# Two pools of landing buffers for weight blocks, used as one rotation in the feed-forward blocks

## The chip, the core and the metric

The kernel runs on one core of one Trainium2 chip. The metric is the device time of one execution in microseconds (us); lower is better. A time is given as the median of several runs. The profile is of one further execution, with times from the start of its first instruction.

## What is computed

The reference is a network of two layers on a sequence of 256 tokens of width 1024, in float32. Each layer is a feed-forward block, a mixer, and a second feed-forward block, each with a norm in front, a norm behind, and a residual sum:

```python
for l in range(DEPTH):                 # DEPTH = 2
    g = norm_g[l]
    h = swiglu(rms_norm(x, g[0, 0]), ffn_w_gate[l, 0], ffn_w_up[l, 0], ffn_w_down[l, 0])
    x = x + 0.5 * rms_norm(h, g[0, 1])
    h = rms_norm(x, g[1, 0])
    ...                                # m = even_mixer(h, ...) for l = 0, odd_mixer(h, ...) for l = 1
    x = x + rms_norm(m, g[1, 1])
    h = swiglu(rms_norm(x, g[2, 0]), ffn_w_gate[l, 1], ffn_w_up[l, 1], ffn_w_down[l, 1])
    x = x + 0.5 * rms_norm(h, g[2, 1])
```

with `swiglu(x, w_gate, w_up, w_down) = (silu(x @ w_gate) * (x @ w_up)) @ w_down` and an inner width of 2816. The even mixer is an attention with compressed keys and a gated recurrence, the odd one a differential attention. The kernel's six stages, in order, are block 0 (feed-forward), block 1 (even mixer), blocks 2 and 3 (feed-forward), block 4 (odd mixer) and block 5 (feed-forward).

## The kernel before

**The tokens and the products.** The 256 tokens are two tiles (`t` = 0, 1) of 128. A float32 product is made of three matmuls: each operand is split into a high part that TensorE takes at full rate and a low part, and `mm3` (lines 291 to 293) adds high x high, low x high and high x low. The first group of a stage does the same in another order (`group_first`, line 339).

**A weight block's way.** The weights lie in DRAM in the order in which they are used, cut into blocks of 128 x 1024 floats (512 KB), 331 of them. `emit_load` emits for each: a DMA by SyncE into a landing buffer `raw` (line 241), a cast by ScalarE (ACT) to the high part `whi` (line 266), a subtraction by VectorE (DVE) for the low part `wlo` (line 271). A landing buffer is free again when both have read it. `whi` and `wlo` lie in a ring of nine pairs in the feed-forward blocks (five of pool `wsp`, four of the block's pool `fw`, in the order `RING`). `fill` keeps up to seven split blocks emitted ahead of the matmuls (`AHEAD_F` + 1). The `wlo` are kept in order by a written dependency.

**A feed-forward block.** The inner width is done in six chunks (`CHUNKS`) of 512, 512, 512, 256, 512 and 512 columns, numbered 0 to 5. A chunk is gate products, then `silu` on ScalarE (line 489) from the two PSUM banks of the gate, then the transposes of the previous chunk's output (line 400), then up products into banks that the `silu` has read, then the down products of the previous chunk. The working banks are four, so the up products cannot start before the `silu`. In block 0, chunk 0's outputs `h` (line 498) and a set of sums over the turned x (`row_sums`, lines 528 to 543) are VectorE's during chunk 1.

**Kept blocks.** Chunks 2 and 4 (`SEVEN`) do gate and up with seven products in place of eight of half size: for these, VectorE forms sums of weight blocks (line 213). Eight blocks of such a chunk are kept for it: B11 (two), then T1, T2 and B21 (two each). A sum overwrites one of its operands (T1 and T2 add to B11's buffers, T3 to T1's, T4 to B21's), so a B11 buffer stays in use up to T4, the sixth of the seven operands (B11, T1, T2, B21, T3, T4, B22).

**The two pools.** `wraw` is opened once and has five landing buffers. Each feed-forward block opens `fraw` with eight (`RAWS`) in `ffn_scope`. Before the change a load is put into `fraw` if its block is one of the kept ones, into `wraw` otherwise:

```python
raw = (wraw if kind is None else state["raws"]).tile([P, SPLIT], F32, name="raw", tag="raw")
moved = nc.sync.dma_start(raw[:, :w], src[:, k * nc_:k * nc_ + w])
```

**What sets the order.** Each engine runs its own instructions in order. Their order is found when the program is built: a scheduler gives an engine, at each step of its own reckoning, the ready instruction that stands first in the program, where a load is ready when its pool has a free buffer and one of the eight DMA semaphores is to be had. So a kept block's load can be issued well before loads that stand ahead of it in the program and have no free buffer. `high_priority` puts some instructions (the splits of transposed values, the norm behind a block) ahead. `late` ties the load of two gains `g` (line 375) behind the loads of blocks 20 and 22.

**When a block's loads count as its own.** `ours` is true for a load whose block is the one whose scope is open. The first four loads of the program are emitted before block 0's scope opens; at the end of a feed-forward block the first loads of the next stage are emitted before its scope opens, and these go to `wraw`. For blocks 2 and 5 the scope opens before the last two blocks of the mixer's output weights, and these count as the feed-forward block's (`MOVED`).

Of the kernel before, what the change touches and what calls it, by code (L numbers as in the profile page):

```python
# [12 lines left out]
F32 = mybir.dt.float32  # L13
# [7 lines left out]
P = 128  # L21
# [14 lines left out]
CHUNKS = [512, 512, 512, 256, 512, 512]  # L36
SEVEN = (2, 4)
RAWS = 8
RING = "wfwfwfwfw"


# [88 lines left out]
def _unit_width(u):  # L130
    return u[3] * sum(b - a for a, b in u[4])
# [51 lines left out]
def forward(ctx, tc, a):  # L183
# [4 lines left out]
    wraw = ctx.enter_context(tc.tile_pool(name="wraw", bufs=5))  # L188
# [13 lines left out]


    SPLIT = 1024
    state = {"i": 0, "off": 0, "block": -1, "pool": None, "first": None, "n": 0, "turn": 0}
    queue = []
    los = []
    late = {}
# [3 lines left out]
    def add(to, what):  # L212
        nc.vector.tensor_tensor(to, to, what, op=ALU.add)  # L213
        return to

    def emit_load():

        if state["i"] >= len(UNITS):
            return
        u = UNITS[state["i"]]
        ours = BLOCK_OF[state["i"]] == state["block"]
        state["i"] += 1
        width = _unit_width(u)
        nk = u[3]
        kind = u[5] if len(u) > 5 else None
        if u[0] is not None:  # L230
            off = state["off"]
            state["off"] += P * width
            src = a["w"][off:off + P * width].rearrange("(p n) -> p n", p=P)
        nc_ = width // nk
        per = max(1, SPLIT // nc_)
        for k in range(0, nk, per):
            n = min(per, nk - k)
            w = n * nc_
            if u[0] is not None:
                raw = (wraw if kind is None else state["raws"]).tile([P, SPLIT], F32, name="raw", tag="raw")  # L240
                moved = nc.sync.dma_start(raw[:, :w], src[:, k * nc_:k * nc_ + w])
                for key in [key for key in late if key <= state["n"]]:
                    after(late.pop(key)(), moved)
            if kind is not None:
                if kind == "T1":
                    kept["B12", k] = raw
                    raw = add(kept["B11", k], raw)
                elif kind == "T2":
                    kept["B22", k] = raw
                    raw = add(kept["B11", k], raw)  # L250
                elif kind == "T3":
                    raw = add(kept["B12", k], kept["B22", k])
                elif kind == "T4":
                    raw = add(kept["B21", k], kept["B11", k])
                elif kind == "B22":
                    raw = kept["B22", k]
                else:
                    kept[kind, k] = raw
            pool, tag = wsp, "w"
            if ours:  # L260
                if RING[state["turn"] % len(RING)] == "f":
                    pool, tag = state["pool"], "f"
                state["turn"] += 1
            hi = pool.tile([P, SPLIT], F32R, name="whi", tag=tag + "hi")
            lo = pool.tile([P, SPLIT], F32R, name="wlo", tag=tag + "lo")
            c = nc.scalar.copy(hi[:, :w], raw[:, :w])  # L266
            if state["first"] is not None:
                if 0 < state["n"] < 16:
                    after(c, state["first"])
            state["n"] += 1  # L270
            state["lo"] = nc.vector.tensor_tensor(lo[:, :w], raw[:, :w], hi[:, :w].bitcast(F32), op=ALU.subtract)  # L271
            if los:
                after(state["lo"], los[-1])
            los.append(state["lo"])
            queue.append((hi[:, :w].rearrange("p (k n) -> p k n", k=n), lo[:, :w].rearrange("p (k n) -> p k n", k=n), n, u[2] + k))
# [27 lines left out]
    def fill():  # L303
        ahead = 3 if state["pool"] is None else state["ahead"]
        while len(queue) < ahead + 1 and state["i"] < len(UNITS):
            if state["i"] in MOVED and BLOCK_OF[state["i"]] != state["block"]:
                break
            emit_load()
# [69 lines left out]
    def after(b, a_):  # L378

        tc.add_manual_dep(b.ins, a_.ins.name, mybir.DependencyInfo(mybir.DependencyClass.NoSync, mybir.DependencyReason.SCHED_ONLY), reason="order")  # L380
# [85 lines left out]
    def ffn_scope(block):  # L466

        fx = ExitStack()
        state["pool"] = fx.enter_context(tc.tile_pool(name="fw", bufs=BUFS_F))
        state["block"] = block  # L470
        state["ahead"] = AHEAD_F
        fp = fx.enter_context(tc.tile_pool(name="fp", bufs=2))
        fr = fx.enter_context(tc.tile_pool(name="fr", bufs=4))
        state["tmp"] = lambda: fp.tile([P, 512], F32, name="tmp", tag="h")
        state["raws"] = fx.enter_context(tc.tile_pool(name="fraw", bufs=RAWS))
        state["turn"] = 0
        return fx, fp, fr

    def ffn(scope, r, turn1, gpost, gnext, at=None):
# [788 lines left out]
    with tc.tile_pool(name="pre", bufs=1) as pre:  # L1268
        lb = pre.tile([P, 512], F32, name="lb")
        lbm = pre.tile([P, 512], F32, name="lbm")  # L1270
        with tc.tile_pool(name="rt", bufs=1) as rt:
            angles, tables = rope_tables(rt, tabm, tabd)
            bounds = even_prep(lb, lbm)
            side.extend([None] * 24 + [angles, None, None, tables, None, bounds])
            r, turn1 = ffn(ffn_scope(0), r, turn1, gpost, gnext, FIRST_AT)
        gpost, gnext = load_g(0, 1, 1), load_g(0, 2, 0)
        second = even(r, turn1, tabm, lb, lbm)
    scope = ffn_scope(2)
    r, turn1 = second(gpost, gnext)
    r, turn1 = ffn(scope, r, turn1, load_g(0, 2, 1), load_g(1, 0, 0))  # L1280
    r, turn1 = ffn(ffn_scope(3), r, turn1, load_g(1, 0, 1), load_g(1, 1, 0))
    gpost, gnext = load_g(1, 1, 1), load_g(1, 2, 0)
    second = odd(r, turn1, tabd)
# [31 lines left out]
```

## Time and profile before

| | us |
|---|---|
| median of 3 runs | 1024.93 |
| lowest and highest run | 1020.07, 1025.9 |
| the profiled execution | 1024.06 |
| its span, first to last instruction | 1022.3 |

The span is that of the profiled execution alone, 1.8 us less than the execution's own time. TensorE is busy for 98% of it, VectorE for 77%, ScalarE for 57%. A busy share says little here; what matters is where TensorE stands still, and what ended that wait. In the rows below the engines are PE (TensorE, matmuls), ACT (ScalarE), DVE (VectorE), POOL (GpSimd) and SP (SyncE; SPq is its queue, which issues DMAs). L266 is line 266 of the kernel. Idle time in square brackets stands before the instruction, with the last of the things it waited for.

### The profile page before, as it was taken

To read this page: it belongs to the slowest core of one execution; us is meant where nothing else is said; L and a number is where in the kernel's file an instruction comes from. 1 tells how busy PE (TensorE), PEld (TensorE's weight loads), DVE (VectorE), ACT (ScalarE), POOL (GpSimd) and SP (SyncE) were. 2 spreads that over 40 slices of the span, in tenths; PEclk is the share of its full clock that TensorE was granted. 3 is DMA by queue.
4 is the path that set the end of the run, shared out by engine and by line. 5 is a ranking of instruction groups with operands and counts; after the bars stand their busy time and mean duration, and the time that the engine had idled before them with its cause. 6 is when DMAs were issued, how large, how long until landed. Compare 5 with 4: busy or idle time off the path is not lost.

```text
span 1022.3 us, 13231 instructions
## 1 busy us (share of the span) xinstructions
PE 996.9 (98%) x4883; PEld 828.4 (81%) x4883; DVE 789.9 (77%) x1068; ACT 584.1 (57%) x846; POOL 52.1 (5%) x61
## 2 busy tenths in 40 slices
PE   7899999999999999999999999999999989999997
PEld 6778988888788788898888789888877868889886
DVE  5888997579468789888668988865776769988852
ACT  5547575468544664747447474653665657474741
POOL 1000000022101100000000000000001200000000
PEclk8999999999899999999999999999999999999999
DMA  8948317275222873925936383494734347392431
GB/s 313 307 153 296 115 66 271 86 264 186 96 83 84 295 261 115 316 84 184 330 117 234 124 289 123 134 324 146 245 109 146 118 143 259 101 308 75 141 127 41
DMA packets 51905, 184.26 MB, mean 180 GB/s; under 512 B 6136, under 2 KB 6528, under 8 KB 51840
## 3 DMA queue, kind: packets, MB, share of 16 engines
q1 hardware_dynamic: 48960, 176.05, 50.6%
q10 hardware_dynamic: 2880, 7.37, 2.0%
q8 instruction: 38, 0.62, 0.2%
q14 instruction: 27, 0.22, 0.1%
HBM read 182.35 MB, written 1.05 MB: 179 GB/s over the span
## 4 chain that ended last, share of the span: by engine, by line
PE 84%; DVE 7%; ACT 3%; issue 3%; DMA 2%; POOL 1%; SPq 0%; DVEq 0%; POOLq 0%; ACTq 0%
PE w L291 15%; PE w L293 15%; PE w L292 15%; PE y L291 9%; PE y L293 9%; PE y L292 9%; PE w L339 6%; DMA raw<-in_w_dram 2%; DVE wlo L271 2%; PE w L400 2%; ACT whi L266 1%; PE y L400 1%; POOL pm L1153 1%; DVE E L1003 0%; PE y L929 0%
## 5 line engine op out<-in xcount | busy, mean ns | idle before, releaser
L266 ACT CAST whi<-raw 128x1024 fp32r<-128x1024 f32 (+2 forms) x379 | 392.8, 1049 | 289.2 <-PE y L293 85.1
L271 DVE TENSOR_TENSOR wlo<-raw,whi 128x1024 fp32r<-128x1024 f32 (+2 forms) x379 | 456.6, 1225 | 104.3 <-ACT whi L266 99.9
L291 PE MATMUL w<-whi,xThi 128*128 128x512 f32 (+1 forms) x676 | 254.4, 376 | 5.5 <-ACT s L489 5.5
L293 PE MATMUL w<-whi,xTlo 128*128 128x512 f32 (+1 forms) x676 | 250.8, 371 | 0.0
L292 PE MATMUL w<-wlo,xThi 128*128 128x512 f32 (+1 forms) x676 | 250.7, 371 | 0.0
L291 PEld LDWEIGHTS w<-whi,xThi 128*128 128x128 f32 x676 | 128.3, 190 | 27.9 <-ACT s L489 6.0
L293 PEld LDWEIGHTS w<-whi,xTlo 128*128 128x128 f32 x676 | 128.3, 190 | 22.4 <-issue 0.3
L292 PEld LDWEIGHTS w<-wlo,xThi 128*128 128x128 f32 x676 | 128.5, 190 | 20.8
L291 PE MATMUL y<-whi,hThi 128*128 128x512 f32 x352 | 138.6, 394 | 0.0
L293 PE MATMUL y<-whi,hTlo 128*128 128x512 f32 x352 | 137.4, 390 | 0.0
L292 PE MATMUL y<-wlo,hThi 128*128 128x512 f32 x352 | 137.4, 390 | 0.0
L213 DVE TENSOR_TENSOR raw<-raw 128x1024 f32<-128x1024 f32 x64 | 77.4, 1221 | 1.0
L293 PEld LDWEIGHTS y<-whi,hTlo 128*128 128x128 f32 x352 | 66.1, 188 | 14.4
L292 PEld LDWEIGHTS y<-wlo,hThi 128*128 128x128 f32 x352 | 66.1, 188 | 13.5
L291 PEld LDWEIGHTS y<-whi,hThi 128*128 128x128 f32 x352 | 66.1, 188 | 13.5
L408 DVE TENSOR_TENSOR hTlo<-w,hThi 128x512 fp32r<-128x512 f32 (+1 forms) x48 | 29.8, 641 | 28.3 <-ACT hThi L407 27.9
L339 PE MATMUL w<-whi,xThi 128*128 128x512 f32 (+2 forms) x124 | 39.6, 397 | 5.5 <-ACT xThi L407 5.5
L435 POOL TENSOR_TENSOR sm<-sm,mhalf 128x1 f32<-128x1 f32 x12 | 6.6, 550 | 713.2 <-DVE sm L433 713.2
L407 ACT CAST hThi<-w 128x512 fp32r<-128x512 f32 (+1 forms) x48 | 25.2, 553 | 24.5 <-PE w L400 24.5
L339 PE MATMUL w<-wlo,xThi 128*128 128x512 f32 (+2 forms) x124 | 37.7, 389 | 0.8 <-DVE wlo L271 0.8
L339 PE MATMUL w<-whi,xTlo 128*128 128x512 f32 (+2 forms) x124 | 37.9, 387 | 0.0
L489 ACT ACTIVATE s<-w,sm 128x512 f32<-128x512 f32 (+1 forms) x40 | 25.5, 645 | 13.1 <-PE w L293 12.6
(276 smaller groups left out, 1161.9 us busy)
## 6 DMA issues: line engine op xcount, KB each, us to landing
raw<-in_w_dram SPq DMA_DIRECT2D x325, 512.0 KB, 5.3
g<-in_norm_g_dram ACTq DMA_DIRECT2D x9, 512.0 KB, 5.4
raw<-in_w_dram SPq DMA_DIRECT2D x4, 448.0 KB, 3.3
g<-in_norm_g_dram SPq DMA_DIRECT2D x2, 512.0 KB, 7.9
out_dram<-x SPq DMA_DIRECT2D x4, 256.0 KB, 2.1
E<-in_hw_dram ACTq DMA_DIRECT2D x1, 576.0 KB, 6.4
x<-in_x_dram SPq DMA_DIRECT2D x2, 256.0 KB, 3.2
x<-in_x_dram SPq DMA_DIRECT2D x1, 512.0 KB
```

What stands on the lines that cost most here:

```text
L213: nc.vector.tensor_tensor(to, to, what, op=ALU.add)
L266: c = nc.scalar.copy(hi[:, :w], raw[:, :w])
L271: state["lo"] = nc.vector.tensor_tensor(lo[:, :w], raw[:, :w], hi[:, :w].bitcast(F32), op=ALU.subtract)
L291: mm(ps, hi[:, j, :], rhi, start=start, stop=False, skip_group_check=again)
L292: mm(ps, hi[:, j, :], rlo, start=False, stop=False, skip_group_check=again)
L293: state["mm"] = mm(ps, lo[:, j, :], rhi, start=False, stop=stop, skip_group_check=again)
L339: state["mm"] = mm(o, lhs[:, k, :], rhs[:, i, :], start=j == 0 and k == 0, stop=j == 2 and k == KD - 1)
L400: nc.tensor.transpose(ps[:, i * P:(i + 1) * P], src[:, (b + i) * P:(b + i + 1) * P], ident)
L407: c = nc.scalar.copy(h2, ps)
L408: return c, nc.vector.tensor_tensor(lo.rearrange("p a b -> p (a b)"), ps, h2.bitcast(F32), op=ALU.subtract)
L489: nc.scalar.activation(s[:, :w], ps[:, :w], AF.Silu, scale=r[t])
L1153: nc.gpsimd.tensor_tensor(pm[:, 1, :, :], pm[:, 1, :, :], rl.unsqueeze(2).broadcast_to([P, n, nk]), op=ALU.mult)
```

## The change

In a feed-forward block the loads are counted from the opening of its scope (`rawn`). Of each thirteen, the first five go to `wraw` and the next eight to `fraw`, whether a block is kept or not. Loads that are not the block's own go to `wraw`, as before. The pools have the sizes that they had.

```diff
--- before.py
+++ after.py
@@ -36,6 +36,7 @@
 CHUNKS = [512, 512, 512, 256, 512, 512]
 SEVEN = (2, 4)
 RAWS = 8
+RAWS_W = 5
 RING = "wfwfwfwfw"
 
 
@@ -202,7 +203,7 @@
 
 
     SPLIT = 1024
-    state = {"i": 0, "off": 0, "block": -1, "pool": None, "first": None, "n": 0, "turn": 0}
+    state = {"i": 0, "off": 0, "block": -1, "pool": None, "first": None, "n": 0, "turn": 0, "rawn": 0}
     queue = []
     los = []
     late = {}
@@ -237,7 +238,9 @@
             n = min(per, nk - k)
             w = n * nc_
             if u[0] is not None:
-                raw = (wraw if kind is None else state["raws"]).tile([P, SPLIT], F32, name="raw", tag="raw")
+                in_f = ours and state["rawn"] % (RAWS + RAWS_W) >= RAWS_W
+                state["rawn"] += ours
+                raw = (state["raws"] if in_f else wraw).tile([P, SPLIT], F32, name="raw", tag="raw")
                 moved = nc.sync.dma_start(raw[:, :w], src[:, k * nc_:k * nc_ + w])
                 for key in [key for key in late if key <= state["n"]]:
                     after(late.pop(key)(), moved)
@@ -473,7 +476,7 @@
         fr = fx.enter_context(tc.tile_pool(name="fr", bufs=4))
         state["tmp"] = lambda: fp.tile([P, 512], F32, name="tmp", tag="h")
         state["raws"] = fx.enter_context(tc.tile_pool(name="fraw", bufs=RAWS))
-        state["turn"] = 0
+        state["turn"] = state["rawn"] = 0
         return fx, fp, fr
 
     def ffn(scope, r, turn1, gpost, gnext, at=None):
```

## Rows read from the trace of the kernel before

**Rows 1.** The profile's page: the head of the page, and the first line of its part 1 (busy us, share of the span, instructions).

```profile
span 1022.3 us, 13231 instructions
...
PE 996.9 (98%) x4883; PEld 828.4 (81%) x4883; DVE 789.9 (77%) x1068; ACT 584.1 (57%) x846; POOL 52.1 (5%) x61
```

**Rows 2.** The list of waits, TensorE (PE) alone, its two largest entries: who waited, on what line, for whom: us in total, times, longest us.

```profile
PE w L291 <- ACT s L489: 5.5, 2, 4.2
PE w L339 <- ACT xThi L407: 5.5, 2, 4.0
```

**Rows 3.** Busy time by windows of 10 us: stretch, its length, then busy us (instructions) of PE, PE's weight loads, VectorE (DVE), ScalarE (ACT) and GpSimd (POOL), TensorE's granted clock, DMA share, GB/s.

```profile
10.00:20.00 10.00, 9.39 (x34) 7.17 (x35) 8.92 (x11) 6.13 (x9) 1.37 (x1) 0.71 1.03 419
40.00:50.00 10.00, 8.26 (x41) 6.61 (x39) 8.89 (x11) 3.79 (x5) 0.00 (x0) 1.00 0.89 291
50.00:60.00 10.00, 7.49 (x26) 5.99 (x27) 6.66 (x7) 5.16 (x7) 0.00 (x0) 0.83 1.00 390
380.00:390.00 10.00, 10.00 (x50) 8.34 (x49) 10.00 (x12) 6.87 (x10) 0.00 (x0) 1.00 0.62 202
```

**Rows 4.** The timeline of TensorE in block 0, chunk 1, from the transposes of the gate outputs on: start us, us, engine, line, operation, out<-in, form, count [idle before <- releaser].

```profile
47.22 1.03 PE L400 MATMUL w<-ident,h 128*128 128x128 f32 x8
52.51 0.50 PE L291 MATMUL w<-whi,xThi 128*128 128x512 f32 x1 [4.25 <-ACT s L489]
...
56.97 0.39 PE L291 MATMUL w<-whi,xThi 128*128 128x512 f32 x1
```

**Rows 5.** The timeline of ScalarE (ACT) in the same place of block 0, and in that of block 3; columns as before.

```profile
50.82 1.04 ACT L266 CAST whi<-raw 128x1024 fp32r<-128x1024 f32 x1 [5.13 <-DMA raw<-in_w_dram]
51.77 1.26 ACT L489 ACTIVATE s<-w,sm 128x512 f32<-128x512 f32 x2
...
565.98 1.05 ACT L266 CAST whi<-raw 128x1024 fp32r<-128x1024 f32 x1 [3.36 <-PE w L400]
566.93 1.26 ACT L489 ACTIVATE s<-w,sm 128x512 f32<-128x512 f32 x2
```

**Rows 6.** The tile `raw` in the first 51 us, its casts: how many, ns min/median/max, start of the first and of the last, forms.

```profile
L266 ACT CAST whi<-raw x20: 1037/1047/1056, 8.6 to 50.8; 128x1024 fp32r<-128x1024 f32 x20
```

**Rows 7.** The chain that ended last, in order of time, one piece of it: start us, us, what.

```profile
44.41 6.31 DMA raw<-in_w_dram
```

**Rows 8.** The list of waits, SyncE's DMA queue (SP) alone, from 39.6 to 44.8 us.

```profile
SPq L241 <- DVE wlo L271: 4.8, 1, 4.8
```

**Rows 9.** The timeline of VectorE (DVE): block 0 from 26 to 50 us, the sums T4 of block 0's chunk 4, and block 3 from 540 to 550 us.

```profile
26.54 5.76 DVE L271 TENSOR_TENSOR wlo<-raw,whi 128x1024 fp32r<-128x1024 f32 x5 [0.80 <-ACT whi L266]
...
38.21 0.74 DVE L498 SCALAR_TENSOR_TENSOR h<-w,sm,s 128x512 f32<-128x512 f32 x1
...
43.14 5.76 DVE L271 TENSOR_TENSOR wlo<-raw,whi 128x1024 fp32r<-128x1024 f32 x5
...
140.58 2.36 DVE L213 TENSOR_TENSOR raw<-raw 128x1024 f32<-128x1024 f32 x2
...
543.00 5.77 DVE L271 TENSOR_TENSOR wlo<-raw,whi 128x1024 fp32r<-128x1024 f32 x5
```

**Rows 10.** The DMA issues of 12.6 to 13 us and of 562 to 563 us, in this order: out<-in, queue, operation, count, KB each, us from issue to landing.

```profile
raw<-in_w_dram SPq DMA_DIRECT2D x1, 512.0 KB, 7.3
...
raw<-in_w_dram SPq DMA_DIRECT2D x1, 512.0 KB, 3.8
```

**Rows 11.** The timeline of TensorE in the same place as rows 4, in block 2 and in block 3.

```profile
383.41 1.04 PE L400 MATMUL w<-ident,h 128*128 128x128 f32 x8
384.20 0.47 PE L291 MATMUL w<-whi,xThi 128*128 128x512 f32 x1
...
387.05 0.39 PE L291 MATMUL w<-whi,xThi 128*128 128x512 f32 x1
...
565.35 1.03 PE L400 MATMUL w<-ident,h 128*128 128x128 f32 x8
567.67 0.50 PE L291 MATMUL w<-whi,xThi 128*128 128x512 f32 x1 [1.28 <-ACT s L489]
```

**Rows 12.** The timeline of SyncE's queue (SPq): the first 9 us, the load issued at 12.70, and the load of block 3 issued at 562.13.

```profile
1.65 1.37 SPq L241 DMA_DIRECT2D raw<-in_w_dram  x3
...
3.77 3.06 SPq L241 DMA_DIRECT2D raw<-in_w_dram  x3
8.78 0.33 SPq L375 DMA_DIRECT2D g<-in_norm_g_dram  x1
...
12.70 0.33 SPq L241 DMA_DIRECT2D raw<-in_w_dram  x1
...
562.13 0.33 SPq L241 DMA_DIRECT2D raw<-in_w_dram  x1
```

**Rows 13.** The timeline of TensorE at the start of block 5.

```profile
838.13 0.60 PE L400 MATMUL y<-ident,xg 128*128 128x128 f32 x4
...
841.98 0.50 PE L339 MATMUL w<-whi,xThi 128*128 128x512 f32 x1 [1.52 <-ACT xThi L407]
```

**Rows 14.** The timeline of ScalarE in block 0 behind chunk 4, and at the start of block 5.

```profile
150.09 2.94 ACT L266 CAST whi<-raw 128x1024 fp32r<-128x1024 f32 x3
...
839.36 1.05 ACT L266 CAST whi<-raw 128x1024 fp32r<-128x1024 f32 x1 [2.91 <-DMA raw<-in_w_dram]
...
841.36 0.56 ACT L407 CAST xThi<-y 128x512 fp32r<-128x512 f32 x1
```

## The prediction

> **What bounds the kernel now.** I read the page first. Of the 1022.3 us span TensorE (PE) is busy 996.9 us [rows 1], so a change that touches only loads can give back at most some of the other 25.4 us, and what a slow TensorE clock cost. The list of what TensorE waited for says how little of this belongs to weights: the two largest entries are a `silu` (`s`, L489), 5.5 us in two places, and the turned x (`xThi`, L407), 5.5 us in two [rows 2]. No entry names a DMA, so a late load can only show through another engine. The windows then place the largest wait: TensorE is short of full in 40:50 and 50:60, and in the second the granted clock is 0.83 [rows 3].
>
> The largest place is in block 0, the first feed-forward block. After eight transposes from 47.22 TensorE stands 4.25 us, until 52.51, "for ACT s". It then runs slowly for some 4 us: twelve matmuls later it is 56.97 [rows 4], and the clock of [rows 3] lies between the levels of 1.2 and 2.4 GHz. So what is late? ScalarE stands idle 5.13 us before the cast at 50.82, for a DMA, and runs the two `silu` right behind that cast [rows 5]. It takes its instructions in order: the `silu` had its input when the gate group ended, just before the transposes at 47.22, and stood behind a cast whose block had not landed. That cast is the twentieth [rows 6], so its block is load 19 (counted from 0), the last of chunk 0's down blocks. The chain shows its DMA: issued at 44.41, landed 6.31 us later [rows 7]. SyncE had waited 4.8 us for a `wlo` before it could issue [rows 8]. That `wlo` was late because VectorE did the gate outputs and row sums from 38.21 on and came back to splitting at 43.14 [rows 9]. The chain is: VectorE late, one of five `wraw` buffers free late, load 19 issued late, ScalarE blocked, TensorE idle.
>
> **The change, part by part.** Sizes of pools stay. In a feed-forward block load i now takes its buffer from the same pool as load i-13: five `wraw`, eight `fraw`. Before, a load that is not kept waited for the cast and `wlo` of the fifth such load before it, while the eight `fraw` buffers held blocks of a chunk that came much later. No instruction of any engine is added or removed: 331 loads, 379 casts and 379 `wlo` stay. What moves is when SyncE may issue.
>
> *Block 0.* Four loads are emitted before the scope opens (to `wraw`); loads 4 to 8 take `wraw`, 9 to 16 `fraw`, 17 to 21 `wraw`. Load 19's buffer then frees with load 6 or so, whose `wlo` is among the five that VectorE does from 26.54 to 32.3 [rows 9], some 12 us ahead of 44.41. Even the 7.3 us that a load takes behind a full queue [rows 10] end before 40. The `silu` can follow the end of the gate group. What that place then costs, block 2 shows, where the last load came just in time: transposes at 383.41, next matmul at 384.20, and the thirteenth matmul starts at 387.05, 3.64 us after the transposes began [rows 11]. In block 0 the same twenty-one instructions take from 47.22 to 56.97, 9.75 us [rows 4]. Gain 9.75 - 3.64 = 6.1 us, clock included.
>
> *Block 3.* The same place: transposes at 565.35, next matmul at 567.67, "for ACT s" [rows 11]. SyncE issued the load at 562.13 [rows 12], ScalarE cast it at 565.98 and ran `silu` at 566.93 [rows 5]. (The view puts that cast's idle time down to a transpose; a load issued at 562.13 that takes 3.8 us [rows 10] lands at 565.9, so it was the DMA.) The load thirteen before it has its `wlo` among the five from 543.00 to 548.8 [rows 9], so the rotation has the buffer free over 13 us earlier. Gain (567.67 - 565.35) - (384.20 - 383.41) = 1.5 us.
>
> *Block 5.* At 841.98 TensorE has waited 1.52 us for `xThi`; the transposes that this needs began at 838.13 [rows 13]. ScalarE ran it at 841.36, 2.0 us after it began a cast for whose load it had stood idle 2.91 us, until 839.36 [rows 14]; a square lies between. In the rotation the fourth to eleventh feed-forward loads of this block take `fraw`, which is free since block 3, so this one is there early. The square and `xThi` can then be done at about 840.4, when TensorE wants them. I take 1.5 us; the bounds are 0, if the scheduler puts other casts in front, and the 1.52 of the row.
>
> *Block 2* has no wait of this kind, with TensorE at 10.00 in window 380:390 [rows 3]: nothing. *Loads of kept blocks* come later than now, since nothing is reserved for them; they have their turn in order, and I cost this at nothing because the casts of `whi` run in order and are held by the ring of nine `whi`/`wlo` pairs. The cover is worked out under the rivals. *The gains `g`* that `late` ties to blocks 20 and 22 are issued after those blocks, thus later; they are used at the end of block 0, over 100 us on.
>
> Sum: 6.1 + 1.5 + 1.5 = 9.1 us. The profiled execution took 1024.06 us (1022.3 span and 1.8 around it): 1024.06 - 9.1 = 1015.0. The median shown is 0.9 above it, so I say **1016.0 us**, with 1013 to 1019.5 as this case's own range (up: all of block 3's and 5's gain and a quarter of block 0's lost to a new order; down: the other waits for `xThi` in [rows 2] shrink too).
>
> **The rivals.**
>
> *A. Ring order at the start.* Loads 9 to 16 have free buffers from the start, and the scheduler gives SyncE whatever is ready. Already now six loads are out by 6.9 us, with five `wraw` buffers, and at 8.78 the `g` that is tied to block 20 [rows 12]: a kept block and the `g` go ahead of load 5. The load issued at 12.70 takes 7.3 us [rows 10, 12]. The Trainium skill ("DMA: Bandwidth & Descriptors", section "Queues, rings and completion order") says that each DMA engine consumes a ring's descriptors in order, so a block not yet wanted stands before one that is; the trace agrees, 7.3 us here against 3.8 on a quiet queue. At the 419 GB/s of window 10:20 [rows 3] a block of 512 KB (0.524 MB) is 1.25 us. If all eight of `fraw` went ahead instead of some three transfers, load 5 would land 5 x 1.25 = 6.3 us later; with no slack on TensorE's side all of it is lost, and the result is 1016.0 + 6.3 = 1022. Against it: the same eight free buffers let only a few ahead before.
>
> *B. Hidden anyway.* The loads come early, but the place in block 0 waits for something else, such as VectorE's five splits from 43.14 [rows 9], or a new order of the casts brings as many new waits: 1022 to 1027. For it: VectorE is busy 8.9 of 10 there [rows 3]. Against it: block 2 has VectorE at 10.00 in the same place, and TensorE at 10.00 [rows 3].
>
> *C. The rotation waits for kept blocks, and the kernel is slower.* Load i+13 needs the buffer of a kept block B11, which is free only after the sum T4. In chunk 4 of block 0 these sums run from 140.58 to 142.9 [rows 9]. The loads that inherit (53, 54) land 3.8 to 6.3 us later [rows 7, 10], at 146 to 149, and their casts are now at about 151 and 152 (the second and third of three from 150.09 [rows 14]): 2 to 5 us of slack. If the sums come more than this later, TensorE is held at each of eight such chunks. With 3 us at each, 1024.06 - 9.1 + 24 = 1039; it decides for slower from (9.1 + 5.1)/8 = 1.8 us at each. Against it: the loads before them, thirteen deep, leave the casts more in hand than five did.
>
> *D. Half.* Block 0's stall shrinks, but `silu` or the row sums stand behind casts that now find their data: 1019 to 1022.
>
> **How the numbers follow.** Forecast 0.60; A 0.05; D 0.12; B 0.13; C 0.10. What this kernel's measurement can tell from no change is about 0.5%, 5.1 us; its three runs lie 5.8 apart. Below 1019.8 (1024.93 less 5.1) lie the forecast and a little of D: faster 0.65. Between are A, B and the rest of D: same 0.25. Slower 0.10. The range takes the forecast's low side, with what is left of the `xThi` waits gone too, and reaches up through A, D and half of B: 1012 to 1024.5.
>
> **What would show it.** After the change: no TensorE gap over 0.5 us for `s` L489, the clock at 1.00 in 50:60, and the thirteenth matmul 3.6 to 4 us after the transposes of chunk 1; ScalarE's waits for `raw` between 20 and 60 us nearly gone; SyncE with no wait for a `wlo` of 4 us between 30 and 50; the gap near 842 under 0.5 us, some 8 us earlier. Wrong if a gap for `wlo` or `raw` L213 appears behind chunks 2 and 4 (C), if TensorE stands at 20 to 28 us (A), or if the gap in block 0 stays with another releaser (B).

## The result, and the profile after

The changed kernel took 1012.49 us, the median of 6 runs (1009.94 to 1014.87), against 1023.21 us for 6 runs of the kernel before (1020.07 to 1025.90): ratio 0.9895, 95% interval 0.9869 to 0.9921. The prediction was 1016.0 us, range 1012 to 1024.5, with 0.65 on "faster by over 0.5%". So the time lies inside the range near its low end, 3.5 us below the point and 0.5 us below the 1013 to 1019.5 given as the case's own range. A second measurement beside other runs of the kernel before gave 1012.85 us and 0.9903 (0.9881 to 0.9925). One run of e4 (2560.54 us) and one of e6 (1416.37 us), experiments told below, lay far outside all others, and medians and ratios are without them.

The profiled execution took 1009.94 us. The page of the kernel after, span and busy time of each engine, which answers to [rows 1]:

```profile
span 1008.2 us, 13275 instructions
...
PE 990.5 (98%) x4883; PEld 825.0 (82%) x4883; DVE 788.4 (78%) x1068; ACT 583.4 (58%) x846; POOL 52.2 (5%) x61
```

TensorE runs the same 4883 matmuls, VectorE and ScalarE the same counts; TensorE stands idle 17.7 us of its span instead of 25.4. The list of what TensorE waited for, kernel after, its largest entry and the fourth (who waited for whom: us in total, times, longest us), against [rows 2]:

```profile
PE w L342 <- ACT xThi L410: 3.9, 2, 2.9
...
PE y L294 <- ACT xThi L410: 1.4, 1, 1.4
```

The entry for `s` (5.5 us in two places) is gone. That for `xThi` is smaller, but stays. Of its fall from 5.5 to 3.9 us, 1.1 lie at the start of the program, where this wait was 4.0 us before and lies between 2.5 and 4.4 in all the profiles; the rest is block 5's. The wait for `xThi` at L294 is not new: at the same line (L291 then) it was 0.9 us before. Three lines were added above these places, so L291, L339, L407 and L489 of before are L294, L342, L410 and L492 here. The windows, kernel after (columns as in [rows 3]):

```profile
40.00:50.00 10.00, 10.00 (x49) 8.31 (x48) 10.00 (x14) 7.88 (x11) 0.00 (x0) 1.00 0.86 318
50.00:60.00 10.00, 10.00 (x45) 8.16 (x45) 9.97 (x10) 3.15 (x3) 0.00 (x0) 1.00 0.40 132
```

TensorE is full in both windows, with the granted clock at 1.00 where it was 0.83. The place itself, in the timelines of TensorE and ScalarE of the kernel after, against [rows 4, 5]:

```profile
46.20 1.03 PE L403 MATMUL w<-ident,h 128*128 128x128 f32 x8
46.99 0.48 PE L294 MATMUL w<-whi,xThi 128*128 128x512 f32 x1
...
49.82 0.39 PE L294 MATMUL w<-whi,xThi 128*128 128x512 f32 x1
```

```profile
43.05 2.00 ACT L269 CAST whi<-raw 128x1024 fp32r<-128x1024 f32 x2
45.02 0.69 ACT L492 ACTIVATE s<-w,sm 128x512 f32<-128x512 f32 x1
46.46 0.69 ACT L492 ACTIVATE s<-w,sm 128x512 f32<-128x512 f32 x1 [0.75 <-PE w L296]
```

From the transposes to the thirteenth matmul it is 49.82 - 46.20 = 3.62 us; it was 9.75. The cast of the twentieth block is the second of the two at 43.05, and before the second `silu` ScalarE now waits for TensorE, not the other way round. Load 19 is the first of the two in this line of the timeline of SyncE's DMA queue:

```profile
27.30 1.46 SPq L244 DMA_DIRECT2D raw<-in_w_dram  x2
```

It landed 6.8 us later, by the list of DMA issues from 27.2 to 28 us (count, KB each, median us to landing), at 34.1 and so ten us ahead of its cast:

```profile
raw<-in_w_dram SPq DMA_DIRECT2D x1, 512.0 KB, 6.8
```

### The profile page after: what moved, and what is told of

The parts are those of the page before. It is cut to its first block, busy times and chain, and to the rows that moved or that the text cites. A ratio compares the mean times of both kernels' runs of the same rounds, so it can differ in the third digit from the quotient of the medians.

```text
span 1008.2 us, 13275 instructions
## 1 busy us (share of the span) xinstructions
PE 990.5 (98%) x4883; PEld 825.0 (82%) x4883; DVE 788.4 (78%) x1068; ACT 583.4 (58%) x846; POOL 52.2 (5%) x61
## 4 chain that ended last, share of the span: by engine, by line
PE 89%; DVE 5%; ACT 2%; issue 1%; POOL 1%; DMA 1%; SPq 0%; POOLq 0%; DVEq 0%; ACTq 0%
PE w L294 16%; PE w L296 16%; PE w L295 16%; PE y L294 9%; PE y L296 9%; PE y L295 9%; PE w L342 7%; DVE wlo L274 2%; PE w L403 2%; PE w L1023 1%; ACT whi L269 1%; PE y L403 1%; DMA raw<-in_w_dram 1%; POOL pm L1156 1%; DVE pm L1158 0%
## 5 line engine op out<-in xcount | busy, mean ns | idle before, releaser
L294 PE MATMUL w<-whi,xThi 128*128 128x512 f32 (+1 forms) x676 | 252.7, 374 | 0.0
L294 PEld LDWEIGHTS w<-whi,xThi 128*128 128x128 f32 x676 | 127.5, 189 | 21.5 <-issue 1.0
L294 PE MATMUL y<-whi,hThi 128*128 128x512 f32 x352 | 138.7, 394 | 0.0
L294 PEld LDWEIGHTS y<-whi,hThi 128*128 128x128 f32 x352 | 66.1, 188 | 13.5
L342 PE MATMUL w<-whi,xThi 128*128 128x512 f32 (+2 forms) x124 | 39.0, 393 | 3.9 <-ACT xThi L410 3.9
L410 ACT CAST hThi<-w 128x512 fp32r<-128x512 f32 (+1 forms) x48 | 25.1, 552 | 24.5 <-PE w L403 24.5
L342 PE MATMUL w<-wlo,xThi 128*128 128x512 f32 (+2 forms) x124 | 37.4, 387 | 0.4 <-DVE wlo L274 0.4
L342 PE MATMUL w<-whi,xTlo 128*128 128x512 f32 (+2 forms) x124 | 37.7, 385 | 0.0
L492 ACT ACTIVATE s<-w,sm 128x512 f32<-128x512 f32 (+1 forms) x40 | 25.9, 647 | 15.8 <-PE w L296 15.6
```

Of the source, the lines that this page charges most:

```text
L294: mm(ps, hi[:, j, :], rhi, start=start, stop=False, skip_group_check=again)
L342: state["mm"] = mm(o, lhs[:, k, :], rhs[:, i, :], start=j == 0 and k == 0, stop=j == 2 and k == KD - 1)
L410: c = nc.scalar.copy(h2, ps)
L492: nc.scalar.activation(s[:, :w], ps[:, :w], AF.Silu, scale=r[t])
```

## Where the time went, in all the kernels

All these kernels issue the same 4883 matmuls, and but for a few stretches in the same order, so the time between two given matmuls can be compared from trace to trace (stretches in which the order differs are taken as a whole, from before them to behind them). The table gives what each kernel gained in such a stretch on the profiled execution of the kernel before, in us (negative: lost): block 0 from the last transpose to the thirteenth matmul behind the transposes of chunk 1; block 3, the same place and a few matmuls more; the way into block 5, from 817 to 854 us of before; and the even mixer from 239 to 332 us of before, which uses no weight of a feed-forward block. Block 2's start, from 356 to 360 us of before, lies outside the forecast's terms; it is taken up in the account of the sum. The ratio is to the runs of the kernel before in the same comparison.

| kernel | median us | ratio (95%) | block 0 | block 2's start | block 3 | into block 5 | mixer |
|---|---|---|---|---|---|---|---|
| changed, first profile | 1012.49 | 0.9895 (0.9869 to 0.9921) | 6.1 | 0.0 | 1.6 | 1.1 | 4.2 |
| changed, again (e1) | 1012.85 | 0.9903 (0.9881 to 0.9925) | 6.1 | 0.0 | 1.6 | 1.0 | 3.0 |
| order on ScalarE (e2) | 1014.05 | 0.9912 (0.9892 to 0.9932) | 6.1 | -0.8 | 1.5 | -1.3 | 4.2 |
| rotation in block 0 (e3) | 1015.28 | 0.9938 (0.9916 to 0.9960) | 6.1 | -1.1 | -0.4 | 0.3 | 4.2 |
| rotation elsewhere (e4) | 1018.53 | 0.9970 (0.9948 to 0.9991) | -1.3 | 0.0 | 1.6 | 1.0 | 4.2 |
| row sums later (e5) | 1018.87 | 0.9957 (0.9934 to 0.9980) | 6.1 | -1.7 | 1.6 | -3.5 | 1.5 |
| eleven buffers (e6) | 1013.58 | 0.9898 (0.9865 to 0.9931) | 6.1 | 0.0 | 1.6 | 1.1 | 3.0 |
| nine buffers (e7) | 1012.25 | 0.9895 (0.9863 to 0.9927) | 6.1 | 0.0 | 1.6 | 1.1 | 0.0 |
| square behind xThi (e8) | 1011.49 | 0.9887 (0.9857 to 0.9918) | 6.1 | 0.0 | 1.6 | 1.9 | 3.0 |
| one load (e9) | 1015.06 | 0.9924 (0.9897 to 0.9951) | 6.1 | -0.7 | 0.1 | 0.3 | 4.2 |
| eight buffers (e10) | 1011.93 | 0.9887 (0.9862 to 0.9913) | 6.1 | 0.0 | 1.5 | 1.1 | 3.0 |

In the first pair of profiles the matmuls end 14.1 us earlier, more than the medians differ (10.7). Only 8.8 of this (6.1 + 1.6 + 1.1) lies where the change acts. Another 1.0 lies in the first 16 us and the rest in the mixer; what these are, the experiments had to tell.

## The experiments

The theory: in block 0 one block lands late, and it costs time only because its cast stands ahead of `silu` in ScalarE's queue; the rotation helps by letting that one load start early. Against it stood that the gain comes from loads running further ahead in general, that the mixer's clock follows from block 0's hole, and that the depth of the rotation counts.

**e1: the changed kernel again.** No edit.

> The changed kernel once more, beside the kernel before on the same chip, and a second profile. Its first profile is 14.1 us shorter than that of before, of which 6.1 lie in block 0, 1.5 in block 3, 1.1 in block 5, but also 1.0 in the first 14 us and about 4 in the even mixer (238 to 370 us of before), where the change moves nothing that I can see and where the granted clock of before was lower (0.71 in 10:20, 0.75 in 260:270). Theory (the late load's cast stood ahead of silu on ScalarE): 8.7 us are the change's, ratio 0.9915, and the pieces at the start and in the mixer come and go with the granted clock: at least one of them differs from the first profile. Rival (the change brings the clock of the mixer too, since TensorE arrives without the earlier hole): ratio 0.9865 to 0.9885 and the mixer again at full clock.

Block 0, 3 and 5 gave the same within 0.1 us; the mixer 3.0 instead of 4.2. Ratio 0.9903, between the two forecasts, its interval holding the first (0.9915) and only the edge of the second; the later runs settle the mixer.

**e2: only ScalarE's order.** Pools as before.

```diff
             c = nc.scalar.copy(hi[:, :w], raw[:, :w])
+            if state["hold"] is not None:
+                after(c, state["hold"])
...
-                nc.scalar.activation(s[:, :w], ps[:, :w], AF.Silu, scale=r[t])
+                state["silu"] = nc.scalar.activation(s[:, :w], ps[:, :w], AF.Silu, scale=r[t])
...
+                state["hold"] = state["silu"] if ci == 1 else None
                 group(pu, xT, w)
+                state["hold"] = None
```

> Pools as before (eight and five); only ScalarE's order changes: the casts that belong to chunk 1's up group are put behind the chunk's last silu, in every feed-forward block, so that the cast of the late load no longer stands ahead of it (18 casts before the silu in block 0, where before has 20). The load itself stays as late. Theory (the late load costs only because its cast stands ahead of silu): the hole in block 0 goes from 4.25 us to under 1 us and the one in block 3 from 2.3 to under 1 us, 6 to 7.6 us in all, ratio about 0.993; block 5 keeps its wait for xThi. Rival (the lateness itself is what costs, the down group wants the block soon after): TensorE then waits at the down blocks instead and less than half is won, ratio 0.997 or above.

The load was as late as before: issued at 44.61 us (44.41 in [rows 7]) and landed 4.6 us later, at 49.2, after both `silu`. The list of DMA issues for that moment and the timelines of ScalarE and TensorE, kernel e2:

```profile
raw<-in_w_dram SPq DMA_DIRECT2D x1, 512.0 KB, 4.6
```

```profile
45.65 0.69 ACT L491 ACTIVATE s<-w,sm 128x512 f32<-128x512 f32 x1 [2.80 <-PE w L295]
47.09 0.69 ACT L491 ACTIVATE s<-w,sm 128x512 f32<-128x512 f32 x1 [0.74 <-PE w L295]
...
48.62 3.91 ACT L266 CAST whi<-raw 128x1024 fp32r<-128x1024 f32 x4
```

```profile
46.83 1.03 PE L402 MATMUL w<-ident,h 128*128 128x128 f32 x8
47.62 0.48 PE L293 MATMUL w<-whi,xThi 128*128 128x512 f32 x1
```

The block is cast behind `silu`, as the second of the four from 48.62, and TensorE has no hole: 6.1 and 1.5 us won, what the rotation wins there within 0.1. So lateness alone costs nothing here; the place in the queue costs. The down blocks were not missed. The rival falls. In block 5 this kernel lost 1.3 us: the wait of before was there (1.2 us), and the granted clock fell to 0.66 in 830:835 behind it, which it had not done in the profile of before.

**e3 and e4: the rotation in block 0 alone, and in the others alone.** The edit is the change's, with a condition:

```diff
                 in_f = ours and state["rawn"] % (RAWS + RAWS_W) >= RAWS_W
+                if state["block"] not in ROTATE:
+                    in_f = kind is not None
                 state["rawn"] += ours
```

with `ROTATE = (0,)` in e3 and `(2, 3, 5)` in e4.

> The rotation of thirteen in block 0 alone; blocks 2, 3 and 5 keep eight and five. Theory: block 0's 6.1 us and nothing else, ratio 0.994; the holes at block 3 (2.3 us) and block 5 (1.5 us) stay. Rival (the gain is spread, because ScalarE's 49 us of waits for loads shrink everywhere): under 3 us here. Second rival (the mixer's clock follows from block 0's hole): 9 to 10 us here, ratio 0.990, with the mixer behind it at full clock.

> The rotation of thirteen in blocks 2, 3 and 5; block 0 keeps eight and five. Theory: 1.5 us in block 3 and 1.1 in block 5, 2.6 us, ratio 0.9975; block 0 keeps its 4.25 us for silu. Rival (spread gain): more than 5 us here. Second rival (the mixer's clock is block 0's doing): the mixer at 238 to 370 us is as slow here as in the kernel before.

Ratios 0.9938 and 0.9970, as the theory had them, to 0.0005; 6.2 and 3.0 parts in a thousand add up to 9.2, against 9.7 and 10.5 for the whole change. The gain is not spread. Kernel e4, TensorE's timeline in block 0 and in block 3:

```profile
46.48 1.03 PE L406 MATMUL w<-ident,h 128*128 128x128 f32 x8
53.02 0.79 PE L297 MATMUL w<-whi,xThi 128*128 128x512 f32 x1 [5.52 <-ACT s L495]
...
561.66 1.03 PE L406 MATMUL w<-ident,h 128*128 128x128 f32 x8
562.45 0.48 PE L297 MATMUL w<-whi,xThi 128*128 128x512 f32 x1
```

Block 0 keeps its hole (5.5 us in this execution), block 3 has lost its. And the second rival of e3 falls by e4: with block 0 as before, the mixer ran at full clock. The window in which the mixer's slow stretch lies, in the kernel before:

```profile
260.00:270.00 10.00, 10.00 (x32) 6.57 (x30) 3.23 (x8) 5.57 (x13) 1.04 (x1) 0.75 0.05 21
```

The same window in e4, where block 0 still has its hole:

```profile
260.00:270.00 10.00, 10.00 (x43) 6.56 (x41) 4.17 (x11) 7.06 (x19) 1.04 (x1) 1.00 0.25 86
```

And the window that answers to it in e7 (nine buffers, below), which comes to this place 6 us earlier since block 0's hole is closed:

```profile
250.00:260.00 10.00, 9.95 (x34) 7.66 (x34) 3.04 (x6) 4.61 (x13) 1.04 (x1) 0.66 0.43 143
```

The granted clock stands ahead of the last two numbers: 0.75, 1.00 and 0.66. With the hole open the mixer was slow (before) and fast (e4), with the hole closed it was fast (the changed kernel) and slow (e7). So block 0's hole does not decide the mixer's clock, and the 3 to 4 us there are not counted as the change's. Whether the slow stretch comes more rarely after the change isn't shown: only two profiles (before and e4) have the hole.

**e5: the row sums later.** The first link of the chain, VectorE. The sums are those over the turned x (`row_sums`).

```diff
             h = [gated(t, pu[t], s[t], w) for t in range(NT)]
-            sums.extend(row_sums(fp))
...
                 h = [gated(t, pu[t], s[t], w) for t in range(NT)]
+                if ci == 1:
+                    sums.extend(row_sums(fp))
```

> Pools as before (eight and five). The row sums of chunk 0's down product, which VectorE did between 38.21 and 43.14 us together with the gate outputs, are written out after chunk 1's gate outputs instead, in each feed-forward block, so that VectorE splits three blocks more before them and the raw buffers come free earlier. Theory (the first link of the chain: VectorE late, so a buffer late, so load 19 late): load 19 is issued some 4 to 5 us earlier than 44.4, lands before 47, and the hole of 4.25 us in block 0 shrinks to under 1 us: 4 to 6 us, ratio 0.994 to 0.996. Rival (the queue or the number of buffers holds load 19 back whatever VectorE does): the hole stays above 3 us, ratio 0.998 or above.

VectorE split one block at 37.77 and three from 39.56 on, ahead of the rest of the sums, from 42.96 on, and SyncE issued load 19 at 39.01 instead of 44.41. The timeline of VectorE, and then that of SyncE's queue, kernel e5:

```profile
37.77 1.22 DVE L271 TENSOR_TENSOR wlo<-raw,whi 128x1024 fp32r<-128x1024 f32 x1
...
39.56 3.49 DVE L271 TENSOR_TENSOR wlo<-raw,whi 128x1024 fp32r<-128x1024 f32 x3
42.96 0.69 DVE L532 TENSOR_TENSOR xf<-xf 128x512 f32<-128x512 f32 x1
```

```profile
39.01 0.33 SPq L241 DMA_DIRECT2D raw<-in_w_dram  x1
```

It landed 5.5 us later, at 44.5, and the hole is gone: 6.1 us in block 0. The link holds. But the same edit made a new wait in block 2, where `silu` now stands behind casts of the row sums (`oThi`, `Shi`) that come later; TensorE's timeline there:

```profile
377.38 1.03 PE L400 MATMUL w<-ident,h 128*128 128x128 f32 x8
379.94 0.50 PE L291 MATMUL w<-whi,xThi 128*128 128x512 f32 x1 [1.52 <-ACT s L489]
```

and the way into block 5 lost 3.5 us, with a clock of 0.81 in 830:840. Ratio 0.9957: inside the forecast, and a worse repair than the rotation.

**e6, e7, e10: eleven, nine and eight buffers.** The changed kernel with `RAWS = 6`, `4` and `3` beside `RAWS_W = 5`.

> One rotation as in the changed kernel, but of eleven buffers (six and five): two fewer blocks in reserve. Theory (what is needed is that the last down block of chunk 0 doesn't wait for a split done after VectorE's gate outputs; eleven blocks earlier is early enough): the same time as with thirteen within 2 us, ratio to before 0.989 to 0.992. Rival (the depth itself is worth time, kept blocks holding eight of eleven leave too few): 3 us or more slower than thirteen, with new waits for a split behind chunks 2 and 4.

> One rotation of nine buffers (four and five), while a chunk of the seven-product kind keeps up to eight blocks. This is the price of the case that the prediction feared, that the rotation waits for kept blocks. Theory: block 0's hole at 47 stays closed, as load 19 takes the buffer of load 10, split by 32 us; but behind chunks 2 and 4 the next loads wait for the sums (in the changed kernel the last sums of chunk 2 run at 66.96 and 69.35 us, and the first down block behind them is cast at 73.12, so a load of 3.8 us just comes in time; in chunk 4 the sums run until 135.7 and two down blocks are cast at 128.23 and 129.18, so these come late): 0 to 2 us at each chunk 2, 2 to 6 us at each chunk 4, four blocks, so 8 to 32 us slower than thirteen, 1020 to 1045 us. Rival (nine are enough, since the buffers are handed out as they come free): as thirteen within 2 us.

> One rotation of eight buffers (three and five), as many as the blocks that a chunk of the seven-product kind keeps, so no load behind such a chunk can start before its sums. With nine the load behind chunk 2 was issued at 69.00 and the one behind chunk 4 at 131.31 us (after 19 and 28 us of waiting), that block landed at 134.69 and was cast at 134.95 instead of 129.18, and TensorE did not wait. Theory (the slack behind these chunks is used up between nine and eight, since one more block comes after the sums): waits of 0.5 to 4 us of TensorE for wlo or whi behind chunk 4, in up to four blocks, 2 to 12 us slower than nine. Rival (even so the splits are ahead of TensorE): as nine within 1.5 us.

All three are as fast as thirteen: 0.9898, 0.9895, 0.9887. For eleven this was the theory; for nine and eight it was not. The loads do wait for the kept blocks, as feared. The list of waits of SyncE's DMA queue in the kernel with eight, first from 45 to 70 us, then from 95 to 135:

```profile
SPq L244 <- DVE raw L214: 20.9, 2, 18.5
```

```profile
SPq L244 <- DVE wlo L274: 28.3, 2, 27.6
```

SyncE stands 18.5 us in chunk 2 and 27.6 us in chunk 4. These waits are not the smaller rotation's, though: with thirteen its longest waits there are 18.5 and 27.6 us too, and in the kernel before they were 21.1 and 30.2. What the number of buffers sets is how many blocks are on their way when SyncE has to stand: with thirteen the first load behind the two waits is the 34th and the 54th to be issued, with eight the 29th and the 49th, five blocks nearer to their use.

TensorE hardly noticed. Its list of waits has no entry between 90 and 170 us, and in the windows of this kernel (e10) it is short of full between 130 and 140 us, by 0.07 us:

```profile
130.00:140.00 10.00, 9.93 (x45) 7.75 (x44) 5.40 (x7) 6.45 (x8) 0.00 (x0) 1.00 0.59 210
```

Matched by matmuls, eight lost 0.5 us there, in block 0 alone, and nine nothing. So my expectation of 8 to 32 us for nine was wrong by all of it. I had taken the time of a cast for the time at which it was needed. With thirteen, load 48, the first of chunk 4's two down blocks, is cast at 128.23, and TensorE takes it at 138.32: some 9 us in hand. With eight that is used up. Load 48 is issued at 132.98, behind the first of the last two sums, lands at 138.28, and TensorE takes its high part as soon as the cast is done. The timelines of ScalarE and TensorE, kernel e10:

```profile
138.30 2.00 ACT L269 CAST whi<-raw 128x1024 fp32r<-128x1024 f32 x2 [0.35 <-DMA raw<-in_w_dram]
...
138.93 0.40 PE L294 MATMUL w<-whi,xThi 128*128 128x512 f32 x1
139.40 1.18 PE L294 MATMUL y<-whi,hThi 128*128 128x512 f32 x4
```

The loss stays small because the order of the program has other matmuls to put there: one of the operand T4 stands ahead of the down block (138.93), and the four with its high part ahead of those with the low part, which VectorE makes from 139.38 on. So the theory for eight, that the slack ends between nine and eight, holds at this one place, and its price of 2 to 12 us doesn't.

**e8: the square behind the turned x.** The changed kernel and one order more.

```diff
-            return lambda: to_T(xg[:, i * 512:(i + 1) * 512], xT[t], 4, 4 * i, ybank)
+            def go():
+                done = to_T(xg[:, i * 512:(i + 1) * 512], xT[t], 4, 4 * i, ybank)
+                if t == 1:
+                    after(state["sq"], done[0])
+                return done
+            return go
...
-        sq = nc.scalar.activation(junk, x[t], AF.Square, scale=1.0 / 32, accum_out=ss)
+        state["sq"] = sq = nc.scalar.activation(junk, x[t], AF.Square, scale=1.0 / 32, accum_out=ss)
```

> The changed kernel, and ScalarE's square of the second half of x (for the next block's norm) put behind the casts of the turned x (xThi) of that half, where it stood ahead of them. Theory (what is left of the wait near 832 us is this square, 1.06 us, ahead of xThi): the wait of 0.96 us there goes, 0.7 to 1.5 us in all with the like places of other blocks, ratio to before 0.988 to 0.991, not to be told from thirteen by its times but by its trace. Rival (xThi waits for the product that feeds the transposes, on VectorE): the wait stays, with the square moved.

First the place in the changed kernel, the timeline of ScalarE and, last line, of TensorE:

```profile
830.75 1.06 ACT L421 ACTIVATE junk<-x 128x1024 bf16<-128x1024 f32 x1 [3.18 <-DVE x L444]
...
831.81 0.56 ACT L410 CAST xThi<-y 128x512 fp32r<-128x512 f32 x1
...
832.43 0.50 PE L342 MATMUL w<-whi,xThi 128*128 128x512 f32 x1 [0.96 <-ACT xThi L410]
```

The timeline of ScalarE in the same place of e8:

```profile
833.54 0.59 ACT L410 CAST xThi<-y 128x512 fp32r<-128x512 f32 x1 [3.25 <-PE y L403]
...
837.29 0.58 ACT L410 CAST xThi<-y 128x512 fp32r<-128x512 f32 x1
837.76 1.06 ACT L426 ACTIVATE junk<-x 128x1024 bf16<-128x1024 f32 x1
```

In the changed kernel ScalarE had been free for 3.18 us, then took the square, whose x VectorE had just finished, and the turned x stood behind it. In e8 `xThi` runs when its transposes are there, the square last, and the entry for `xThi` at this place is gone from TensorE's waits; the way into block 5 gains 1.9 instead of 1.1. The theory holds at this place. Its "0.7 to 1.5 us in all" isn't shown: at the start of block 3 the same profile loses 1.0 us against the changed kernel, where ScalarE stands 3.59 us for a load and `xThi` is cast behind it. As e6 and e7 lose 0.4 and 0.6 us in that place without this edit, whether the new order brings that late load is open. By its runs, 0.9887, e8 can't be told from the changed kernel; 1 us is a thousandth.

**e9: one load.** The kernel before, in which load 19 alone takes a `fraw` buffer:

```diff
-                raw = (wraw if kind is None else state["raws"]).tile(
+                raw = (wraw if kind is None and state["n"] != 19 else state["raws"]).tile(
```

> The kernel before with a single load changed: load 19 of block 0, the last down block of chunk 0, takes one of the eight fraw buffers, which is free from the start; all other loads, the order on ScalarE and the blocks 2, 3 and 5 stay as they are. Theory (this one load is all of block 0's gain): the hole of 4.25 us closes to under 0.5 us, block 0 is 6.1 us shorter, ratio 0.994, as with the rotation in block 0 alone. Rival (the loads around it matter as well: load 18 is nearly as late, it landed at 44.55 in the kernel before): a wait of 1 us or more stays at the same place, 3 to 5 us in all.

The timelines of ScalarE and TensorE, kernel e9, in block 0:

```profile
44.76 2.00 ACT L266 CAST whi<-raw 128x1024 fp32r<-128x1024 f32 x2 [1.77 <-DMA raw<-in_w_dram]
46.66 1.36 ACT L489 ACTIVATE s<-w,sm 128x512 f32<-128x512 f32 x2
...
47.07 1.03 PE L400 MATMUL w<-ident,h 128*128 128x128 f32 x8
47.86 0.48 PE L291 MATMUL w<-whi,xThi 128*128 128x512 f32 x1
```

ScalarE still waits 1.77 us for load 18, and it does no harm: the `silu` follow at 46.66, and TensorE goes from the transposes to the next matmul (47.86) without a wait. The single load is worth block 0's whole 6.1 us; block 3, untouched, keeps its wait for `s` (1.23 us before the matmul at 557.92). Ratio 0.9924, with 0.9938 for the rotation of block 0 inside the interval.

## Why the prediction was right, point by point

**The chain.** Shown link by link: splits earlier on VectorE close the hole (e5), the one buffer closes it (e9), and the order on ScalarE closes it with the load as late as ever (e2). The Trainium skill ("Perfetto Trace Analysis", section "Tensor Engine Instruction (MATMUL, LD_WEIGHTS)") says in passing that ScalarE, VectorE and GpSimd are strictly first in, first out; the traces agree, 5.13 us of standing at a cast in [rows 5] with a `silu` ready behind it, and none in e2.

**Block 0**, forecast 6.1 by taking block 2's passage of the same place: 9.75 - 3.62 = 6.1 us, and the same in every kernel that closed the hole.

**Block 3**, forecast 1.5: 1.6.

**Block 2**, forecast nothing. In chunk 1, the place that the prediction read, this holds. The start of the block was left out, and there it doesn't: see the sum.

**Block 5**, forecast 1.5, measured 1.1 net, and by another account. The wait of 1.52 us at 841.98 [rows 13] is 0.96 us at 832.43 after the change, and two waits for `wlo` just ahead of it (0.17 and 0.29 us) are gone. The step that failed is "the square and `xThi` can then be done at about 840.4": it took the load to be all that held the square. With the load early, ScalarE stands free for 3.18 us and the square waits for x, from VectorE; `xThi` stands behind the square (e8 takes this away). And at a turn some 23 us earlier (818.64 us before, 806.55 after) two casts that now find their data stand ahead of an `xThi`, where one stood before: TensorE's wait there went from 0.85 to 1.35 us. That is what rival D feared, in small. Of the sum of these, 0.56 + 0.46 - 0.50 = 0.5, to the 1.1 measured some is scatter: e3 and e9, which have the old order there, come out 0.3 ahead too. "The gap near 842 under 0.5 us" was a miss.

**The sum**, forecast 9.1: 8.8 found where it was put. The two comparisons give 10.7 and 9.8 us between the medians, and 8.8 (ratio 0.9914) lies inside both intervals. That 1016.0 was 3.5 us too high has two parts. First, it was built on the median of three runs, 1024.93; the six runs of the comparison give 1023.21, 1.7 us less, which no step of the reasoning could know. Second, the medians differ by 1 to 2 us more than 8.8, and a part of this has a place: the step "*Block 2* has no wait of this kind: nothing".

At the start of block 2 the same thing happens as at that of block 5: ScalarE stands for a load, and `xThi` is cast right behind that block. In the profile of before this came just in time. In the other four profiles with the old pools in this block (e2, e3, e5, e9) it came too late, and TensorE lost 0.7 to 1.7 us (column "block 2's start"). In none of the seven with the rotation there does ScalarE stand for a load at this place; `xThi` waits for its transposes, and nothing is lost. The timelines of ScalarE: before, then e3, then the changed kernel:

```profile
353.90 1.05 ACT L266 CAST whi<-raw 128x1024 fp32r<-128x1024 f32 x1 [0.91 <-DMA raw<-in_w_dram]
354.90 0.59 ACT L407 CAST xThi<-y 128x512 fp32r<-128x512 f32 x1
...
345.14 1.05 ACT L272 CAST whi<-raw 128x1024 fp32r<-128x1024 f32 x1 [2.35 <-DMA raw<-in_w_dram]
346.10 0.58 ACT L413 CAST xThi<-y 128x512 fp32r<-128x512 f32 x1
...
343.45 0.59 ACT L410 CAST xThi<-y 128x512 fp32r<-128x512 f32 x1 [1.48 <-PE y L403]
```

The way into block 5 is alike: with the old pools it takes from 3.5 us more to 0.3 us less than in the profile of before, with the rotation always 1.0 us less or better. So the profile of before was a mild one in both places, and what is found against it is too little. An estimate from the means of the five profiles with the old pools in these two blocks: 0.9 us more at block 2 and 0.8 us more at block 5, 10.5 us with the 8.8. With one profile of each kernel, and with e2 and e5 changed in more than this, it stays an estimate; scatter of the granted clock may have a share too.

**Rival A** didn't come, and the reason given holds: three blocks (loads 9 to 11) went out ahead of load 5, where before two and a `g` had. Load 5 took 7.2 us as before, and ScalarE's wait at its cast was 2.67 us against 2.72:

```profile
19.51 1.05 ACT L269 CAST whi<-raw 128x1024 fp32r<-128x1024 f32 x1 [2.67 <-DMA raw<-in_w_dram]
```

**Rival B** is excluded by the trace, TensorE being full from 40 to 60 us.

**Rival C**, the slower side, was too dear at 0.10 and its price was wrong. In the changed kernel the load that I had feared for (53) was issued at 129.79, ahead of the sums at 133.38, landed at 133.0 and was cast at 143.83: some 10 us of slack, not 2 to 5. "Load i+13 needs the buffer of a kept block" fails as a step: within a pool a load gets whatever buffer has come free. The load at 129.79 went out when VectorE had split the first block of T3 (at 129.73), before VectorE had come to the sums of T4. And where fewer buffers made blocks come later, with nine and eight, TensorE lost nothing and 0.5 us.

**The signs.** ScalarE has no wait for a DMA between its cast at 19.51 and 218 us, as said. "SyncE with no wait for a `wlo` of 4 us between 30 and 50" was wrong: it has one of 5.7 us there, and one of 18.5 for a sum behind it (21.1 in the kernel before), both harmless, as the blocks are not wanted yet. A wait of SyncE is no sign of a loss until ScalarE stands at that block with something urgent behind.

## What to carry to other kernels

When an engine that works in order stands at a data-dependent instruction, look at what is queued behind it: a late transfer costs not by its own lateness but by the urgent instruction that stands behind its consumer, and reordering the consumer can be worth nearly as much as bringing the data early (0.9912 against 0.9903 here). Buffers reserved for a later stage are idle buffers: handing them out in turn let eight do better than thirteen in two reserves, though with eight the slack was used up in one place. And don't read the time of an instruction that follows its data as the time when it is needed; the slack is seen at the engine that consumes it last. A wait that is harmless in one profile can cost in the next: compare more than one profile of the kernel before.

## What the runs showed of the hardware that I had not expected

The granted clock of one and the same stretch differs between profiles, also where the kernels don't differ, by an amount as large as the changes measured here. In the even mixer TensorE was granted 0.75 in 260:270 in the kernel before and 1.00 in e4; by the matched matmuls the stretch was 3.1 us shorter in nine of the eleven profiles that followed, as slow as before in e7, and halfway in e5. In the slow stretch ten matmuls in a row started 0.2 us further apart each. At the start, too, the kernels lie from 1.1 us earlier to 0.5 us later than the profile of before by 16.5 us, with the new pools in block 0 (-1.1 to +0.5) as with the old (-0.8 to -0.2), so the 1.0 us of the first pair says nothing on the change. What decides the clock there is open. The practical side is that two single profiles, 14.1 us apart, overstate this change by 3 to 4 us against the medians over several runs. Matched stretches show where the time lies, but they too stand on the one execution of the kernel before that was profiled.
